# The y products of a pair of groups in the two halves of TensorE's columns, and GLU low parts built by DMA, in an S5 + MoBA trunk

## The chip, the core and the metric

The kernel runs on one core of one Trainium2 chip. The metric is the device time of one execution in microseconds. All times of rows are microseconds from the start of the profiled execution's span. PE is TensorE (PEld its weight loads), DVE is VectorE, ACT is ScalarE, POOL is GpSimd and SP is SyncE.

## The reference

A trunk of two layers over 256 tokens of width 1024. Each layer is a half-step SwiGLU FFN, a token mixer and a second half-step SwiGLU FFN, each with an RMSNorm ahead and a residual add. The mixer of layer 1 is an S5 state-space layer with 64 groups of 16 channels and 64 complex states; the mixer of layer 2 is block-sparse attention. The change lies in the S5 mixer:

```python
x_re, x_im = coef * (b @ u)                       # per group, complex
_, _, h_re, h_im = lax.associative_scan(combine, (abar, x), axis=1)
y = einsum('bsgp,gcp->bsgc', h_re, c_re) - einsum('bsgp,gcp->bsgc', h_im, c_im)
y = y.reshape(bsz, s, D_MODEL) + d_skip * u
y = gelu(y)
val, gate = split(y @ w_glu, 2, axis=-1)          # w_glu: 1024 x 2048
return val * sigmoid(gate)
```

## The kernel before

All large products are made in three parts: a weight w and an activation x are each split into a rounded part (hi, xh) and the rest (lo, xl), and `mm3` adds hi·xh, lo·xh and hi·xl. The weights lie in HBM as a row of granules of 128 x 1024 (512 KB), in the order in which they are used. `fetch` (line 162) takes the next granule: SP loads raw (L173), ACT rounds it to hi (L174), DVE subtracts to get lo (L175). hi and lo have four buffers each, raw has three. `take` hands a granule to the products and fetches so that three are ahead. Granules 66 to 81 hold w_glu: 66 to 73 are used in the S5 loop, one a pass, and 74 to 81 after it; the loop fetches 69 to 76.

The S5 mixer works on eight blocks b of eight groups. Time is cut in chunks of CL = 4 steps, NJ = 64 chunks. For a block:

- `s5_u`: ACT scales the rows into Hc (L845), PE transposes them to u (L853), ACT copies u in two halves to U (L858), and POOL's queue copies the two halves of the output matrices Om, swapped, to O2 (L861).
- `s5_x`: PE makes xst from U (L872); DVE multiplies with the tables Ct and St (L882 to L885), scans over the chunks (L888), and multiplies again to G1 and G2 (L891, L892).
- `s5_yu` and `s5_y`: PE adds up y, for each of the eight groups three f32 products of 128 rows and 64 columns, with Tm (L902), Om (L912) and O2 (L914). All write partitions 0 to 63 of a PSUM bank. ACT makes Yg from it with Gelu (L919).
- `s5_t`: PE transposes Yg to yT (L930); ACT makes xh of it (L934) and DVE xl (L938).

The blocks are staggered. A pass i of the loop does, on PE: yT of block i-2, xst of block i, y of block i-1, u of block i+1, and then the twelve GLU products of granule 64+i with block i-2. The order on PE and on SP is the order of the program text; ACT, DVE and POOL get theirs from a scheduler with priorities and a few written constraints (`issue_after`). Every engine works in its own order; tiles with few buffers make it wait for the last reader.

Of the kernel before, what the change touches and what calls it, by code (L numbers as in the profile page):

```python
# [10 lines left out]
F32 = mybir.dt.float32  # L11
F32R = mybir.dt.float32r
I32 = mybir.dt.int32
AF = mybir.ActivationFunctionType
ALU = mybir.AluOpType
# [12 lines left out]
GC = 16  # L28
NST = 64
CL = 4  # L30
NJ = SEQ // CL
# [4 lines left out]
PARTS = (2, 2)  # L36
WARM = (20, 2, 2, 8)
URGENT = 400


def ends(defer):
# [96 lines left out]
def yoco(ctx: ExitStack, tc: tile.TileContext, w, x, xt, ng, fg, sng, sd, sp, sb, sc, cst, out):  # L138
    nc = tc.nc
# [10 lines left out]
    def wbank(name):  # L150
        return psw.tile([128, 512], F32, tag="w", name=name)
# [8 lines left out]
    got, state = {}, {"n": 0, "use": 0, "bg": None, "end": NG, "credit": 0}  # L160

    def fetch():
        n = state["n"]
        if n >= NG:
            return
        state["n"] += 1
        raw = ring.tile([128, GR], F32, tag="raw", name="raw", bufs=3)
        hi = ring.tile([128, GR], F32R, tag="hi", name="hi")
        lo = ring.tile([128, GR], F32R, tag="lo", name="lo")
        step = 512 if n < 7 else GR  # L170
        for o in range(0, GR, step):
            s = slice(o, o + step)
            nc.sync.dma_start(raw[:, s], w[n][:, s])  # L173
            state["hi", n] = nc.scalar.activation(hi[:, s], raw[:, s], AF.Copy)  # L174
            state["lo", n] = nc.vector.tensor_tensor(lo[:, s], raw[:, s], hi[:, s].bitcast(F32), op=ALU.subtract)  # L175
        got[n] = (hi, lo)

# [64 lines left out]
    def xt_tiles(h, v=None):  # L242
        p, v = (xtp, "") if v is None else (v, "k")
        return (p.tile([128, 4, SEQ], F32R, tag=f"xh{h}{v}", name=f"xh{h}{v}", bufs=1),
                p.tile([128, 4, SEQ], F32R, tag=f"xl{h}{v}", name=f"xl{h}{v}", bufs=1))
# [7 lines left out]
    def split_scaled(dst, blk, src, gain):  # L253
        h, l = dst
        nc.scalar.activation(h[:, blk, :], src, AF.Copy, scale=gain)
        nc.vector.scalar_tensor_tensor(l[:, blk, :], src, gain, h[:, blk, :].bitcast(F32),  # L256
                                       op0=ALU.mult, op1=ALU.subtract)

    def transposed(xx, h, versions, bank=wbank):
# [11 lines left out]
        for dst, gi in dsts:  # L271
            for bp in range(2):
                for k in range(2):
                    blk = 2 * bp + k
                    with tc.high_priority(offset=URGENT if h else 0):
                        split_scaled(dst, blk, banks[bp][:, k, :], ngt[:, gi, 4 * h + blk:4 * h + blk + 1])
# [6 lines left out]
    def sumsq(ss, xx, h, urgent=False):  # L283
        with tc.high_priority(offset=URGENT if urgent else 0):
            for t in range(2):
                junk = small.tile([128, 512], F32, tag="junk", name="junk", bufs=1)
                nc.scalar.activation(junk, xx[t][h], AF.Square, accum_out=ss[:, 2 * h + t:2 * h + t + 1])
# [4 lines left out]
    def rnorm(ss, urgent=False, out=None):  # L292

        y = rnorm_tile() if out is None else out
        w_ = small.tile([128, 2, 3], F32, tag="rw", name="rw")
        with tc.high_priority(offset=URGENT if urgent else 0):
            for t in range(2):
# [15 lines left out]
    def rnorm_root(m, out, urgent=False):  # L313

        w_ = small.tile([128, 2], F32, tag="rw2", name="rw2")
        with tc.high_priority(offset=URGENT if urgent else 0):
            nc.vector.reciprocal(w_[:, 0:1], m)
# [6 lines left out]
    def ffn(pool, xx, lhs, r, head_mid, extra, tail_mid, tail, defer=DEFER, by_tile=False, late=False, then=None):  # L324
# [57 lines left out]
        def add(t, n, bank=None, c=slice(0, 512)):  # L382
            with tc.high_priority(offset=URGENT):
                src = acc[n][t] if bank is None else bank
                state["add"] = nc.vector.scalar_tensor_tensor(xx[t][n][:, c], src[:, c], 0.5, xx[t][n][:, c],  # L385
                                                              op0=ALU.mult, op1=ALU.add)
# [41 lines left out]
    with tc.manual_schedule(engines={PE, SP}):  # L428
# [5 lines left out]
        for i_ in range(4):  # L434
            raw = xn[i_ // 2][i_ % 2].rearrange("p (k t) -> p k t", k=2)
# [28 lines left out]
        Tm = smat.tile([128, CL, 32 * GC], F32, name="Tm")  # L464
        Om = smat.tile([128, G, CL, GC], F32, name="Om")
# [11 lines left out]
        H = [slice(0, 64), slice(64, 128)]  # L477
# [334 lines left out]


        sw = s5.enter_context(tc.tile_pool(name="sw", bufs=2))
        Gz = []
        for b in range(2):
            g1 = sw.tile([128, 8, NJ], F32, name=f"G1{b}", bufs=1)
            g2 = sw.tile([128, 8, NJ], F32, name=f"G2{b}", bufs=1)
            mt = sw.tile([128, 8, NJ], F32, name=f"Mt{b}", bufs=1)
            for t_ in (g1, g2, mt):  # L820
                nc.gpsimd.memset(t_[:, :, 0:1], 0.0)
            Gz.append((g1, g2, mt))

        Uz = []
        for b in range(3):
            u = sw.tile([128, 4, 2, NJ], F32, name=f"U{b}", bufs=1)
            nc.gpsimd.memset(u, 0.0)
            Uz.append(u)
        yT = [xt_tiles(h, sw) for h in range(2)]
        st = {}  # L830

        def s5_u(b):
            Hc = sw.tile([64, 8, CL, GC], F32, tag="Hc", name="Hc")
            hc = [None, None]
            for s_ in range(CL):
                t, sl = s_ // 2, s_ % 2
                src = xs[t][b // 4][64 * sl:64 * sl + 64, 128 * (b % 4):128 * (b % 4) + 128]
                rs = r[64 * sl:64 * sl + 64, t:t + 1]
                if b == 0 and s_ % 2:
                    hc[1] = V.tensor_scalar(Hc[:, :, s_, :], src.rearrange("p (g c) -> p g c", c=GC), rs, None, op0=ALU.mult)  # L840
                else:
                    with ExitStack() as order:
                        if b > 0:
                            order.enter_context(tc.issue_after(st[b - 1]["ins"]))
                        hc[0] = nc.scalar.activation(Hc[:, :, s_, :], src.rearrange("p (g c) -> p g c", c=GC), AF.Copy,  # L845
                                                     scale=rs)
            if b == 0:
                with tc.issue_after(hc[0].ins), tc.issue_after(hc[1].ins):
                    fetch()
            ub = wbank("u")  # L850
            uv = ub[:, 0:256].rearrange("p (q j) -> p q j", q=4)
            for q in range(4):
                nc.tensor.transpose(uv[:, q, :], Hc[:, 2 * q:2 * q + 2].rearrange("p g s c -> p (g s c)"),  # L853
                                    ident[0:64, 0:64])
            U = Uz[b % 3]
            for g2 in range(2):
                ps = slice(64 * g2, 64 * g2 + 64)
                done = nc.scalar.activation(U[ps, :, g2, :], uv[ps], AF.Copy)  # L858
            O2 = sw.tile([128, 8, CL, GC], F32, tag="O2", name="O2")
            for hh in range(2):  # L860
                nc.gpsimd.dma_start(O2[64 * hh:64 * hh + 64], Om[64 - 64 * hh:128 - 64 * hh, 8 * b:8 * b + 8])  # L861
            st[b] = {"U": U, "O2": O2, "ins": done.ins}

# [31 lines left out]
        def s5_yu(b):  # L895

            U = st[b]["U"]
            yb = wbank("y")
            st[b]["Y"] = Y = yb[0:64].rearrange("p (g f) -> p g f", g=8)
            for g in range(8):  # L900
                pr = 4 * b + g // 2
                nc.tensor.matmul(Y[:, g, :], U[:, g // 2, g % 2, :], Tm[:, :, GC * pr:GC * pr + GC],  # L902
                                 start=g == 0, stop=False)

        def s5_y(b, groups=range(8)):

            if "Y" not in st[b]:
                s5_yu(b)
            Y, O2 = st[b]["Y"], st[b]["O2"]
            g1, g2_, _ = Gz[b % 2]  # L910
            for g in groups:
                nc.tensor.matmul(Y[:, g, :], g1[:, g, :], Om[:, 8 * b + g].rearrange("p t c -> p (t c)"),  # L912
                                 start=False, stop=False)
                nc.tensor.matmul(Y[:, g, :], g2_[:, g, :], O2[:, g].rearrange("p t c -> p (t c)"),  # L914
                                 start=False, stop=g == 7)
            if groups[-1] < 7:
                return
            Yg = sw.tile([64, CL, 8, GC], F32, tag="Yg", name="Yg")
            nc.scalar.activation(Yg.rearrange("p t g c -> p g t c"), Y.rearrange("p g (t c) -> p g t c", c=GC),  # L919
                                 AF.Gelu_apprx_tanh)  # L920
            st[b]["Yg"] = Yg
            if b == 7:
                table(AF.Sigmoid, Yg[:, CL - 1, 7, GC - 1:GC])
# [21 lines left out]
        def last_t():  # L945
            with tc.high_priority(offset=URGENT):
                s5_t(7)
# [118 lines left out]
        for t in range(2):  # L1066
            nc.scalar.activation(ksb[:, t], kv[t][:, 0:256].rearrange("p (h d) -> p h d", h=KVH), AF.Copy,
                                 scale=r[:, t:t + 1])
            nc.scalar.activation(Vt[:, t], kv[t][:, 256:512].rearrange("p (h d) -> p h d", h=KVH), AF.Copy,
                                 scale=r[:, t:t + 1])  # L1070
# [203 lines left out]
```

## Time and profile before

| | us |
|---|---|
| median of 3 runs | 942.59 |
| lowest, highest | 942.35, 946.56 |
| the profiled execution, whole | 942.14 |
| its span | 940.4 |
| PE busy in it | 926.3 |
| DVE busy | 618.6 |
| ACT busy | 500.9 |

The span runs from the first to the last instruction that the profile shows; the profiled execution's time is 1.7 us longer. A product in f32 is two records on PE; one whose operands are rounded parts (fp32r) is one record.

### The profile page before, as it was taken

What the parts mean: (1) busy time and instruction counts of PE and PEld (TensorE: products, weight loads), DVE (VectorE), ACT (ScalarE), POOL (GpSimd) and SP (SyncE); (2) the same over time, 40 slices, a digit from 0 to 9 for tenths busy, and PEclk for the clock granted to TensorE, in tenths of its full rate; (3) what the DMA queues carried; (4) which work ended last, traced back from release to release, by engine and by line L of the source; (5) the groups of instructions that cost most, each with busy time, mean ns of one, the idle gap of its engine ahead of it and who ended that gap; (6) DMA issues with size and microseconds to landing.
All of it is one profiled execution on the core that took longest, in us unless ns stands there. A gap on an engine that the chain in (4) does not pass through costs nothing.

```text
span 940.4 us, 12472 instructions
## 1 busy us (share of the span) xinstructions
PE 926.3 (99%) x4610; PEld 766.7 (82%) x4610; DVE 618.6 (66%) x958; ACT 500.9 (53%) x742; POOL 41.8 (4%) x94
## 2 busy tenths in 40 slices
PE   9999999998999999999999999999999999999996
PEld 6788888887888888888888888888888888888885
DVE  7899988669976645555576555545578664555545
ACT  7544585566655544444466444444566654444444
POOL 0600000021100000000000000000000000000002
PEclk9999999999999999999999999999999999999999
DMA  8757555564335655555555555555552455555551
GB/s 300 229 195 225 186 185 196 168 208 148 118 98 184 195 187 192 182 196 183 183 179 189 183 185 193 187 184 194 183 178 76 160 186 188 187 190 188 188 186 66
DMA packets 49581, 169.93 MB, mean 181 GB/s; under 512 B 5936, under 2 KB 6368, under 8 KB 49520
## 3 DMA queue, kind: packets, MB, share of 16 engines
q1 hardware_dynamic: 46944, 162.33, 52.6%
q0 software_dynamic: 2144, 6.36, 2.4%
q8 instruction: 36, 0.59, 0.2%
q10 hardware_dynamic: 432, 0.45, 0.1%
q14 instruction: 25, 0.20, 0.1%
HBM read 164.46 MB, written 2.56 MB: 178 GB/s over the span
## 4 chain that ended last, share of the span: by engine, by line
PE 95%; DVE 2%; DMA 2%; ACT 1%; issue 0%; SPq 0%; ACTq 0%; DVEq 0%
PE pi L199 16%; PE pi L201 16%; PE pi L200 16%; PE acc L201 9%; PE acc L199 8%; PE acc L200 8%; PE gT L353 2%; PE glu L199 2%; PE glu L200 2%; PE glu L201 2%; DMA raw<-in_w 2%; PE xst L872 1%; PE q L201 1%; PE y L914 1%; PE y L912 1%; PE y L902 1%
## 5 line engine op out<-in xcount | busy, mean ns | idle before, releaser
L175 DVE TENSOR_TENSOR lo<-raw,hi 128x1024 fp32r<-128x1024 f32 (+1 forms) x307 | 368.7, 1202 | 270.0 <-ACT hi L174 269.4
L174 ACT ACTIVATE hi<-raw 128x1024 fp32r<-128x1024 f32 (+1 forms) x307 | 318.9, 1039 | 326.6 <-PE pi L201 180.4
L199 PE MATMUL pi<-hi,xh 128*128 128x512 f32 x704 | 279.2, 397 | 0.4 <-ACT hi L174 0.4
L201 PE MATMUL pi<-hi,xl 128*128 128x512 f32 x704 | 275.0, 391 | 0.0
L200 PE MATMUL pi<-lo,xh 128*128 128x512 f32 x704 | 274.3, 390 | 0.2
L201 PEld LDWEIGHTS pi<-hi,xl 128*128 128x128 f32 x704 | 132.1, 188 | 28.7 <-DVE xl L256 0.5
L199 PEld LDWEIGHTS pi<-hi,xh 128*128 128x128 f32 x704 | 132.3, 188 | 27.5 <-ACT hi L174 1.1
L200 PEld LDWEIGHTS pi<-lo,xh 128*128 128x128 f32 x704 | 132.4, 188 | 27.4 <-DVE lo L175 1.3
L201 PE MATMUL acc<-hi,gl 128*128 128x512 f32 x352 | 137.0, 389 | 1.0 <-DVE gl L357 1.0
L199 PE MATMUL acc<-hi,gh 128*128 128x512 f32 x352 | 137.8, 392 | 0.1
L200 PE MATMUL acc<-lo,gh 128*128 128x512 f32 x352 | 136.8, 389 | 0.0
L201 PEld LDWEIGHTS acc<-hi,gl 128*128 128x128 f32 x352 | 66.1, 188 | 15.3 <-DVE gl L357 1.6
L199 PEld LDWEIGHTS acc<-hi,gh 128*128 128x128 f32 x352 | 66.1, 188 | 13.8 <-ACT gh L356 0.5
L200 PEld LDWEIGHTS acc<-lo,gh 128*128 128x128 f32 x352 | 66.1, 188 | 13.4
L342 ACT ACTIVATE sl<-pi,ry 128x256 f32<-128x256 f32 x88 | 41.8, 475 | 50.3 <-PE pi L201 43.4
L343 DVE SCALAR_TENSOR_TENSOR g<-pi,ry,sl 128x256 f32<-128x256 f32 x88 | 42.0, 480 | 18.1 <-ACT sl L342 17.9
L1233 POOL TENSOR_TENSOR xg<-y,fgb 128x512 f32<-128x512 f32 (+1 forms) x5 | 5.3, 1064 | 657.7 <-DVE y L385 657.6
L357 DVE TENSOR_TENSOR gl<-gT,gh 128x512 fp32r<-128x512 f32 x44 | 30.1, 683 | 0.0
L353 PEld LDWEIGHTS gT<-ctile,g 128*128 128x128 f32 x176 | 21.8, 139 | 5.7
L353 PE MATMUL gT<-ctile,g 128*128 128x128 f32 x176 | 26.3, 272 | 0.0
L356 ACT ACTIVATE gh<-gT 128x512 fp32r<-128x512 f32 x44 | 25.6, 582 | 0.4 <-PE gT L353 0.4
L912 PE MATMUL y<-Om,G 128*64 128x64 f32 x128 | 15.8, 224 | 1.2 <-DVE G L891 1.2
(298 smaller groups left out, 830.5 us busy)
## 6 DMA issues: line engine op xcount, KB each, us to landing
raw<-in_w SPq DMA_DIRECT2D x293, 512.0 KB, 3.3
raw<-in_w SPq DMA_DIRECT2D x14, 256.0 KB, 4.9
O<-Om POOLq DMA_DIRECT2D x16, 128.0 KB, 2.5
y<-in_xt SPq DMA_DIRECT2D x4, 256.0 KB, 5.0
x<-in_x SPq DMA_DIRECT2D x4, 256.0 KB, 4.9
B<-in_sb POOLq DMA_DIRECT2D x4, 256.0 KB, 3.8
C<-in_sc POOLq DMA_DIRECT2D x4, 256.0 KB, 3.0
Tm<-KD POOLq DMA_DIRECT2D x2, 512.0 KB, 5.4
```

What stands on the lines that cost most here:

```text
L174: state["hi", n] = nc.scalar.activation(hi[:, s], raw[:, s], AF.Copy)
L175: state["lo", n] = nc.vector.tensor_tensor(lo[:, s], raw[:, s], hi[:, s].bitcast(F32), op=ALU.subtract)
L199: nc.tensor.matmul(bank, lh, wh, start=first, stop=False)
L200: nc.tensor.matmul(bank, lh, wl, start=False, stop=False)
L201: nc.tensor.matmul(bank, ll, wh, start=False, stop=last)
L342: nc.scalar.activation(sl, banks[t][:, 0:FC], AF.Silu, scale=r[:, t:t + 1])
L343: nc.vector.scalar_tensor_tensor(g, banks[t][:, FC:2 * FC], r[:, t:t + 1], sl, op0=ALU.mult, op1=ALU.mult)
L353: nc.tensor.transpose(bv[:, k, t * 128:t * 128 + 128], gs[t][:, k * 128:k * 128 + 128], ident)
L356: nc.scalar.activation(gh, bv, AF.Copy)
L357: nc.vector.tensor_tensor(gl, bv, gh.bitcast(F32), op=ALU.subtract)
L872: nc.tensor.matmul(xb[:, 128 * q:128 * q + 128], Sm[:, 4 * b + q, :], U[:, q].rearrange("p g j -> p (g j)"), start=True, stop=True)
L912: nc.tensor.matmul(Y[:, g, :], g1[:, g, :], Om[:, 8 * b + g].rearrange("p t c -> p (t c)"), start=False, stop=False)
```

## The change

The y products of the even groups of a block go to partitions 0 to 63 of the bank and those of the odd groups to partitions 64 to 127, which are the two halves of the array's columns. Their order alternates between the halves. Gelu is then two calls. For granules 69 to 76, lo is no longer made by DVE: ACT writes -raw, rounded, into lo, and POOL's queue adds the granule from HBM to it with an accumulating DMA. O2 gets a third buffer. The tiles of the stage are made in another order, and POOL's memsets get a higher priority.

```diff
+BY_DMA = {*range(69, 77)}
...
             nc.sync.dma_start(raw[:, s], w[n][:, s])
+            if n in BY_DMA:
+                nc.scalar.activation(lo[:, s], raw[:, s], AF.Copy, scale=-1.0)
+                nc.gpsimd.dma_start(lo[:, s], w[n][:, s], accum_op=ALU.add)
             state["hi", n] = nc.scalar.activation(hi[:, s], raw[:, s], AF.Copy)
+            if n in BY_DMA:
+                state["lo", n] = state["lo", n - 1]
+                continue
             state["lo", n] = nc.vector.tensor_tensor(lo[:, s], raw[:, s], hi[:, s].bitcast(F32), op=ALU.subtract)
...
+        yT = [xt_tiles(h, sw) for h in range(2)]
+        for z_ in ("M1", "M2", "Z"):
+            sw.tile([128, 8, NJ], F32, tag=z_, name=z_, bufs=1)
         Gz = []
...
-            for t_ in (g1, g2, mt):
-                nc.gpsimd.memset(t_[:, :, 0:1], 0.0)
+            with tc.high_priority(offset=2 * URGENT):
+                for t_ in (g1, g2, mt):
+                    nc.gpsimd.memset(t_[:, :, 0:1], 0.0)
...
-            nc.gpsimd.memset(u, 0.0)
+            with tc.high_priority(offset=2 * URGENT):
+                nc.gpsimd.memset(u, 0.0)
             Uz.append(u)
-        yT = [xt_tiles(h, sw) for h in range(2)]
...
-            O2 = sw.tile([128, 8, CL, GC], F32, tag="O2", name="O2")
+            O2 = sw.tile([128, 8, CL, GC], F32, tag="O2", name="O2", bufs=3)
...
-            st[b]["Y"] = Y = yb[0:64].rearrange("p (g f) -> p g f", g=8)
+            st[b]["Y"] = Y = [yb[h, 0:256].rearrange("p (q f) -> p q f", q=4) for h in H]
             for g in range(8):
                 pr = 4 * b + g // 2
-                nc.tensor.matmul(Y[:, g, :], U[:, g // 2, g % 2, :], Tm[:, :, GC * pr:GC * pr + GC],
-                                 start=g == 0, stop=False)
+                nc.tensor.matmul(Y[g % 2][:, g // 2, :], U[:, g // 2, g % 2, :], Tm[:, :, GC * pr:GC * pr + GC],
+                                 start=g < 2, stop=False)
...
-            for g in groups:
-                nc.tensor.matmul(Y[:, g, :], g1[:, g, :], Om[:, 8 * b + g].rearrange("p t c -> p (t c)"),
-                                 start=False, stop=False)
-                nc.tensor.matmul(Y[:, g, :], g2_[:, g, :], O2[:, g].rearrange("p t c -> p (t c)"),
-                                 start=False, stop=g == 7)
+            for q in range(4):
+                for g in (2 * q, 2 * q + 1):
+                    nc.tensor.matmul(Y[g % 2][:, q, :], g1[:, g, :], Om[:, 8 * b + g].rearrange("p t c -> p (t c)"),
+                                     start=False, stop=False)
+                for g in (2 * q, 2 * q + 1):
+                    nc.tensor.matmul(Y[g % 2][:, q, :], g2_[:, g, :], O2[:, g].rearrange("p t c -> p (t c)"),
+                                     start=False, stop=q == 3)
...
-            nc.scalar.activation(Yg.rearrange("p t g c -> p g t c"), Y.rearrange("p g (t c) -> p g t c", c=GC),
-                                 AF.Gelu_apprx_tanh)
+            for g2 in range(2):
+                nc.scalar.activation(Yg.rearrange("p t (q g) c -> g p q t c", g=2)[g2],
+                                     Y[g2].rearrange("p q (t c) -> p q t c", c=GC), AF.Gelu_apprx_tanh)
```

The y products of block 2 on PE, in the loop's second pass, before (G are the tiles G1 and G2, O is O2; the last two rows alternate for all eight groups):

```order
L930 MATMUL yT<-ctile,Yg 128x64 x4
L872 MATMUL xst<-U_2122,Sm 128x128 x4
L902 MATMUL y<-Tm,U_2126 64x64 x8
L912 MATMUL y<-Om,G_2110 64x64
L914 MATMUL y<-O_2296,G_2111 64x64
L912 MATMUL y<-Om,G_2110 64x64
```

The same place in the changed kernel:

```order
L944 MATMUL yT<-ctile,Yg 128x64 x4
L884 MATMUL xst<-U_2129,Sm 128x128 x4
L915 MATMUL y<-Tm,U_2133 64x64 x8
L926 MATMUL y<-Om,G_2117 64x64 x2
L929 MATMUL y<-O_2300,G_2118 64x64 x2
L926 MATMUL y<-Om,G_2117 64x64 x2
```

The products are the same in number; those of Om and of O2 now come in twos, one for each half of the columns, and nothing else on PE has moved.

One pass on ACT, before, from one Gelu to the next:

```order
L919 ACTIVATE Yg<-y 64x8x4x16
L858 ACTIVATE U_2124<-u 64x4x64 x2
L887 ACTIVATE Mt_2112<-m_173 128x8x63
L845 ACTIVATE Hc<-x_80,ry 64x8x16 x2
L845 ACTIVATE Hc<-x_82,ry 64x8x16 x2
L174 ACTIVATE hi<-raw 128x1024
L934 ACTIVATE xh0k<-yT 128x4x64
L919 ACTIVATE Yg<-y 64x8x4x16
```

The same pass in the changed kernel:

```order
L933 ACTIVATE Yg<-y 64x4x4x16 x2
L870 ACTIVATE U_2131<-u 64x4x64 x2
L899 ACTIVATE Mt_2119<-m_173 128x8x63
L857 ACTIVATE Hc<-x_80,ry 64x8x16 x2
L857 ACTIVATE Hc<-x_82,ry 64x8x16 x2
L176 ACTIVATE lo<-raw 128x1024
L178 ACTIVATE hi<-raw 128x1024
L948 ACTIVATE xh0k<-yT 128x4x64
```

The copy into lo stands ahead of hi, both ahead of xh, and Gelu is two calls. On DVE the row of lo is gone in each pass, and xl, which stood ahead of the next block's first three products with the tables, now stands behind the second of them.

The end of the loop on POOL's queue in the changed kernel (DMA rows are issues; fgb is the final norm's gain, which before stood right behind the last copy of Om):

```order
L177 DMA lo<-in_w 128x1024
L873 DMA O_2701<-Om 64x512 x2
L177 DMA lo<-in_w 128x1024 x3
L1228 DMA fgb<-in_fg 128x1024
L177 DMA lo<-in_w 128x1024
```

The last row is granule 76. POOL's memsets, which stood behind the first two blocks' copies of Om, now stand ahead of them.

## Rows read from the trace of the kernel before

**Rows 1.** The page: the span, the busy time of each engine with its share of the span and its instructions, and the shares of the chain that ended last.

```profile
span 940.4 us, 12472 instructions
PE 926.3 (99%) x4610; PEld 766.7 (82%) x4610; DVE 618.6 (66%) x958; ACT 500.9 (53%) x742; POOL 41.8 (4%) x94
...
PE 95%; DVE 2%; DMA 2%; ACT 1%; issue 0%; SPq 0%; ACTq 0%; DVEq 0%
```

**Rows 2.** Busy time of each engine in the passes of the loop, cut at the first GLU product of each: from and to, length, busy time of each engine (with its instructions), granted clock, share of time that the DMA engines were busy, GB/s.

```profile
core 0: us, PE busy (x) PEld busy (x) DVE busy (x) ACT busy (x) POOL busy (x), PEclk, DMA share, GB/s
...
225.89:233.80 7.91, 7.91 (x79) 6.74 (x77) 7.78 (x11) 5.00 (x11) 1.03 (x3) 1.00 0.70 212
233.80:241.57 7.77, 7.77 (x78) 6.66 (x76) 7.63 (x11) 5.05 (x11) 1.02 (x3) 1.00 0.51 155
...
249.33:257.08 7.75, 7.75 (x78) 6.66 (x76) 6.92 (x10) 5.07 (x11) 1.03 (x3) 1.00 0.37 107
257.08:264.44 7.36, 7.36 (x74) 6.34 (x72) 6.71 (x10) 3.34 (x6) 1.01 (x2) 1.00 0.34 102
264.44:270.74 6.30, 6.30 (x67) 5.38 (x65) 5.49 (x7) 2.18 (x3) 0.00 (x0) 1.00 0.09 36
```

**Rows 3.** The timeline of PE in one pass: start, time covered, line, operation, out<-in, the array's shape, shapes, number of records.

```profile
249.33 0.50 PE L199 MATMUL glu<-hi,xh0k 128*128 128x512 f32 x1
...
252.27 0.46 PE L930 MATMUL yT<-ctile,Yg 64*128 64x64 f32 x4
252.66 1.16 PE L872 MATMUL xst<-U,Sm 128*128 128x128 f32 x8
253.75 1.15 PE L902 MATMUL y<-Tm,U 128*64 128x64 f32 x16
254.73 0.28 PE L912 MATMUL y<-Om,G 128*64 128x64 f32 x2
...
256.48 0.28 PE L914 MATMUL y<-O,G 128*64 128x64 f32 x2
256.69 0.46 PE L853 MATMUL u<-ctile,Hc 64*128 64x64 f32 x4
```

**Rows 4.** The timeline of ACT in the same pass; in brackets the idle time before a row and what ended it.

```profile
249.10 0.59 ACT L919 ACTIVATE Yg<-y 64x512 f32<-64x512 f32 x1 [2.57 <-PE y L914]
249.60 0.76 ACT L858 ACTIVATE U<-u 64x256 f32<-64x256 f32 x2
...
252.56 1.06 ACT L174 ACTIVATE hi<-raw 128x1024 fp32r<-128x1024 f32 x1
253.64 0.66 ACT L934 ACTIVATE xh1k<-yT 128x256 fp32r<-128x256 f32 x1
256.86 0.59 ACT L919 ACTIVATE Yg<-y 64x512 f32<-64x512 f32 x1 [2.56 <-PE y L914]
```

**Rows 5.** The timeline of DVE in the same pass: the granule's lo.

```profile
253.65 1.22 DVE L175 TENSOR_TENSOR lo<-raw,hi 128x1024 fp32r<-128x1024 f32 x1 [0.70 <-ACT hi L174]
```

**Rows 6.** The timeline of PE's weight loads: of the kern products (128 stationary columns, 32 moving ones) while the S5 matrices are built, of one GLU product, and of the y products with Tm.

```profile
122.60 1.99 PEld L697 LDWEIGHTS kern<-CC,E 128*128 128x128 f32 x16
...
249.44 0.19 PEld L200 LDWEIGHTS glu<-lo,xh0k 128*128 128x128 f32 x1
...
253.75 1.01 PEld L902 LDWEIGHTS y<-Tm,U 128*64 128x64 f32 x16
```

**Rows 7.** The timeline ahead of the loop, all engines.

```profile
207.29 1.48 POOL L827 MEMSET U<- 128x512 f32 x3
...
208.14 0.40 ACT L845 ACTIVATE Hc<-x,ry 64x128 f32<-64x128 f32 x1 [0.81 <-DVE ry L310]
208.14 0.70 DVE L840 TENSOR_SCALAR Hc<-x,ry 64x128 f32<-64x128 f32 x1
...
224.55 0.33 PE L914 MATMUL y<-O,G 128*64 128x64 f32 x2
...
225.51 0.46 PE L853 MATMUL u<-ctile,Hc 64*128 64x64 f32 x4
```

**Rows 8.** The timeline at the end of the loop: the last GLU product of granule 71, hi of granule 75, xh of block 6, the first GLU product of granule 72, hi of granule 76, the sigmoid, and the first product that reads lo of granule 76.

```profile
267.09 0.39 PE L201 MATMUL glu<-hi,xl1k 128*128 128x512 f32 x1
...
267.51 1.06 ACT L174 ACTIVATE hi<-raw 128x1024 fp32r<-128x1024 f32 x1 [2.31 <-PE glu L201]
...
268.48 0.62 ACT L934 ACTIVATE xh1k<-yT 128x256 fp32r<-128x256 f32 x1
...
270.74 0.50 PE L199 MATMUL glu<-hi,xh1k 128*128 128x512 f32 x1
...
274.41 1.06 ACT L174 ACTIVATE hi<-raw 128x1024 fp32r<-128x1024 f32 x1 [0.88 <-PE glu L201]
...
276.47 1.28 ACT L986 ACTIVATE sg<-glu 128x512 f32<-128x512 f32 x2 [1.00 <-PE glu L201]
...
282.93 0.39 PE L200 MATMUL glu<-lo,xh0k 128*128 128x512 f32 x1
```

**Rows 9.** DMA issues by line: out<-in, queue, number, KB each, median us from issue to landing.

```profile
O<-Om POOLq DMA_DIRECT2D x16, 128.0 KB, 2.5
...
Tm<-KD POOLq DMA_DIRECT2D x2, 512.0 KB, 5.4
...
fgb<-in_fg POOLq DMA_DIRECT2D x1, 512.0 KB, 5.0
```

More of the change, by code (lines that the diff above doesn't have):

```diff
@@ L898, in s5_yu, with s5_y @@
             yb = wbank("y")
-            st[b]["Y"] = Y = yb[0:64].rearrange("p (g f) -> p g f", g=8)
+            st[b]["Y"] = Y = [yb[h, 0:256].rearrange("p (q f) -> p q f", q=4) for h in H]
             for g in range(8):
                 pr = 4 * b + g // 2
-                nc.tensor.matmul(Y[:, g, :], U[:, g // 2, g % 2, :], Tm[:, :, GC * pr:GC * pr + GC],
-                                 start=g == 0, stop=False)
-        def s5_y(b, groups=range(8)):
+                nc.tensor.matmul(Y[g % 2][:, g // 2, :], U[:, g // 2, g % 2, :], Tm[:, :, GC * pr:GC * pr + GC],
+                                 start=g < 2, stop=False)
+        def s5_y(b):
             if "Y" not in st[b]:
@@ L910, in s5_y @@
             g1, g2_, _ = Gz[b % 2]
-            for g in groups:
-                nc.tensor.matmul(Y[:, g, :], g1[:, g, :], Om[:, 8 * b + g].rearrange("p t c -> p (t c)"),
-                                 start=False, stop=False)
-                nc.tensor.matmul(Y[:, g, :], g2_[:, g, :], O2[:, g].rearrange("p t c -> p (t c)"),
-                                 start=False, stop=g == 7)
-            if groups[-1] < 7:
-                return
+            for q in range(4):
[5 more added lines that the diff above has]
+                                     start=False, stop=q == 3)
             Yg = sw.tile([64, CL, 8, GC], F32, tag="Yg", name="Yg")
-            nc.scalar.activation(Yg.rearrange("p t g c -> p g t c"), Y.rearrange("p g (t c) -> p g t c", c=GC),
-                                 AF.Gelu_apprx_tanh)
+            for g2 in range(2):
+                nc.scalar.activation(Yg.rearrange("p t (q g) c -> g p q t c", g=2)[g2],
+                                     Y[g2].rearrange("p q (t c) -> p q t c", c=GC), AF.Gelu_apprx_tanh)
             st[b]["Yg"] = Yg
```

## The prediction

> **What bounds the kernel now.** I read the page first, then one stage of it more and more closely. The page [rows 1] shows TensorE (PE) busy for 926.3 us of a span of 940.4 us, and 95% of the chain that ended last lies on PE. So time is won only where PE's stream gets shorter, and only as far as no other engine then holds PE up. The change touches one stage, the S5 loop and the little ahead of it. Cut at the first GLU product of each pass [rows 2], the loop shows a first pass of 7.91 us, three alike of 7.77 to 7.75 (the middle one is left out), one of 7.36 and one of 6.30 us, PE busy for the whole of each, at a granted clock of 1.00. VectorE (DVE) follows closely with 7.78 to 5.49 us, ScalarE (ACT) has 5.07 us in a full pass. The loop is PE-bound, with DVE less than a microsecond behind.
>
> One pass on PE [rows 3] reads: twelve GLU products from 249.33, the yT transposes at 252.27, xst at 252.66, the y products from 253.75, the u transposes at 256.69. The 24 y products are 48 records (each f32 product is two): 16 in the Tm row at 253.75, 32 from 254.73 to the pair at 256.48, whose second record ends its place about 0.06 later and leaves the drain before u. That is 2.85 us for 48 records, 59 ns each. ACT in the same pass [rows 4] works without a gap from Yg at 249.10 to the end of xh at 254.30, 5.20 us, and is then idle 2.56 us until y is done. DVE [rows 5] spends 1.22 us on the granule's lo, after waiting 0.70 us for hi.
>
> **The y products.** What sets the 59 ns? The kern product [rows 6] streams only 32 columns but has 128 stationary ones, and its 16 loads take (1.99 - 0.19) / 15 = 120 ns each; y has 64 stationary columns and (1.01 - 0.14) / 15 = 58 ns. The pace goes by the columns loaded, and y loads and uses one half of the array (the shape reads 128*64) while the other half stands still. After the change neighbouring products go to different halves. The two records of one product stay on one half, but the second of one product can run beside the first of the next. No row of before shows two halves at work at once, so the gain has two bounds: nothing, if the halves take their loads in turn (59 ns a record still), or half of 2.85 us, 1.42 us a pass, if they work side by side. I take the second: half of the columns is unused in all 48 records, and a load already runs beside a product (the load at 249.44 lies under the product at 249.33 that lasts 0.50 us [rows 3, 6]), so nothing in these rows makes a load own the whole array. PE's pass would be 7.75 - 1.42 = 6.33 us.
>
> The Trainium skill speaks against this. Its page "TensorE: Matmul & The Clock Gate", section "Part 3: Packing small matmuls — row/col tiling", says that a weight load overlaps products in flight only if the row groups differ; the two halves here share all rows. By that rule the gain is 0 and the kernel stays at 942 us. Read strictly it would also forbid the load at 249.44, which has the same rows as the product above it, so the trace bears it out only in part; "TensorEngine Tiling (Array Packing)", section "Key Properties", says on the contrary that different tiles load and multiply in parallel, which would give the 1.42 us. No run here shows either yet.
>
> **ACT and DVE.** ACT gets the first step of lo, a copy of the shape of hi, 1.06 us. Yg (64x512, 0.59 us) becomes two calls of 64x256; the nearest row is U, two calls of 64x256 in 0.76 us, so +0.17 us (bounds: 0 and +0.59, two calls as long as the old one). ACT's gapless stretch becomes 5.20 + 1.06 + 0.17 = 6.43 us, at most 6.85. DVE loses 1.22 us: 6.92 - 1.22 = 5.70 us. That saves nothing by itself, since PE hid it; but had it stayed, DVE would hold the pass at 6.9 us. So the pass comes to max(6.33, 6.43, 5.70) = 6.43 us: ACT takes over as the bound by a hair. One more wait is to be looked at: xh stands behind lo and hi on ACT, and the next GLU products need it. Like hi now, lo waits for raw and for the end of the GLU products of four granules ago, whose buffer it takes; hi at 267.51 starts right at that end (267.09 + 0.39 [rows 8]). So xh ends some 2.9 us after yT has begun (0.1 + 1.06 + 1.06 + 0.66); PE gets to GLU again after yT, xst, y and u, 0.39 + 1.09 + 1.43 + 0.39 = 3.3 us after yT began. It fits, by 0.4 us. DVE's xl now stands behind two of the next block's products, and ends about when the third GLU record wants it: a tenth of a microsecond at most.
>
> **The sum over the loop.** Pass one: 7.91 - 6.43 = 1.48. The three full passes: 7.75 - 6.43 = 1.32 each, 3.96. The fifth has no Hc on ACT (3.34 us + 1.23 [rows 2]), so PE sets it: 1.42. In the sixth PE has neither xst nor u, and ACT is late: hi starts at 267.51 and xh ends at 269.10 [rows 8]; with lo ahead it ends at 270.16, so GLU starts about 270.26 instead of 270.74: 0.48. Together 7.34 us.
>
> **Before the loop.** The memsets now come ahead of the copies into O2. In before, POOL's memset of U lies at 207.29 to 208.77 and DVE's Hc at 208.14 takes 0.70 us [rows 7], where ACT needs 0.40 for the same shape. u needs both: without the overlap it follows ACT's Hc (end 208.54) instead of DVE's (208.84): 0.3 us. After that DVE sets the pace up to the last G of block 1; from the O products at 224.55 to u at 225.51 about 14 records become 7: 0.4 us. O2's third buffer and the earlier tiles cost nothing: these copies are issued well over a pass ahead.
>
> **The low parts by DMA.** Each is 512 KB through POOL's queue; the nearest row is fgb, same size and queue, 5.0 us [rows 9]. An accumulating transfer also reads its destination; I bound it by 5.0 and by twice that, 10 us, and take 7.5. POOL's queue is in order: each lo issue waits for ACT, and an O2 copy waits behind it that is wanted more than a pass later. In the loop a granule is used about three passes after its lo, over 15 us, so nothing shows. The tight one is granule 76: its lo waits for GLU of granule 72, as hi did at 274.41, ends on ACT at 275.47, and PE wants the sum at 282.93 [rows 8]: 7.46 us for the transfer. 5.0 us: no wait; 10 us: 2.5 us. With 7.5 us: 0. The doubled ACT work there delays the first sigmoid from 276.47 to 276.53 or so: -0.1 us. SP's raw loads now wait for hi, 252.56 + 2 x 1.06 = 254.68 in this pass, where they waited for DVE's lo, 254.87 [rows 4, 5]: 0.
>
> Sum: 7.34 + 0.3 + 0.4 - 0.1 = 7.9 us. The profiled execution took 942.14 us, so 934.2; the median of the three runs stands 0.45 us higher: 934.7. With PE, ACT and DVE so close that some joints will leak a few hundredths each pass, I say **935.0 us**.
>
> **Rivals.** *The halves take turns* (the change doesn't do what it says): PE still needs 7.75 us a pass, DVE's relief is hidden, only 0.3 us before the loop remains: 942 us. For it: no row with two halves. *Half a gain*: records start 45 ns apart, say, because the closest starts of records anywhere in these rows are the 58 ns of y, and something below half of that may bind: 48 x 14 ns = 0.67 us a pass, 4 us, and 0.5 before: 938 us. *The accumulating transfer is slow* (the slower side): its place is granule 76, its price is its duration less 7.46 us. With the halves side by side it eats the whole gain from 15 us on and makes the kernel slower by over 0.5% from 20 us; if the halves take turns, from 12 us. Beyond about 17 us every pass would wait too. At 20 us, 947 to 952 us. Against it: the copies on that queue take 2.5 to 5.4 us [rows 9], and the DMA engines are busy for 0.34 to 0.37 of the later passes [rows 2].
>
> **How the numbers follow.** Side by side: 0.50, own range 932.5 to 937. Half a gain: 0.15. Taking turns: 0.22. Slow transfer: 0.13. The range leaves out the slow transfer and the last few in a hundred below: 932.5 to 943.5. A measurement of this kernel tells 0.5%, 4.7 us, from no change. Below 937.9 lie the first case and the better part of the second: 0.63 faster. Same: turns and the rest of the second, 0.25. Slower: 0.12.
>
> **What would show it.** Right: y records of a pass cover about 1.4 us instead of 2.85, passes of 6.4 to 6.5 us, ACT without its 2.56 us gap, PE with small gaps before GLU. Wrong: y pairs still 0.115 us apart in start (turns), or waits of PE's lo products for the POOL queue, at granule 76 first (slow transfer), or ACT's Yg calls at 0.59 us each, which would give passes of 6.85 us and some 937 us.

## The result and the profile after

| | before | after |
|---|---|---|
| median, us | 942.85 (5 runs, 942.35 to 946.56) | 936.78 (5 runs, 934.61 to 937.4) |
| the profiled execution, whole | 942.14 | 935.26 |
| its span | 940.4 | 933.5 |

The ratio is 0.9925, 95% interval 0.9913 to 0.9938: faster by 0.75%. The forecast was 935.0 us; 936.78 lies inside the range, 1.8 us above the forecast.

The page after, to be held against [rows 1]:

```profile
span 933.5 us, 12494 instructions
PE 919.7 (99%) x4610; PEld 759.2 (81%) x4610; DVE 608.8 (65%) x950; ACT 510.1 (55%) x758; POOL 47.4 (5%) x102
...
PE 97%; DVE 1%; ACT 1%; DMA 0%; issue 0%; ACTq 0%; DVEq 0%
```

PE is busy for 6.6 us less and the span is 6.9 us shorter. DVE lost 9.8 us, ACT gained 9.2. The passes, cut as in [rows 2]; the last row is the sixth pass:

```profile
core 0: us, PE busy (x) PEld busy (x) DVE busy (x) ACT busy (x) POOL busy (x), PEclk, DMA share, GB/s
226.06:232.44 6.38, 6.38 (x78) 5.26 (x77) 5.04 (x8) 6.22 (x13) 2.13 (x5) 1.00 0.91 205
232.44:239.05 6.61, 6.61 (x78) 5.27 (x76) 6.42 (x10) 6.29 (x13) 2.01 (x4) 1.00 1.05 298
239.05:245.56 6.51, 6.51 (x78) 5.19 (x77) 6.05 (x9) 6.29 (x13) 2.02 (x4) 1.00 0.98 262
245.56:251.91 6.35, 6.35 (x78) 5.23 (x76) 5.73 (x9) 6.20 (x13) 2.00 (x3) 1.00 0.91 211
251.91:258.00 6.09, 6.09 (x74) 4.87 (x72) 5.79 (x9) 4.59 (x8) 0.89 (x1) 1.00 0.93 181
258.00:263.75 5.75, 5.44 (x68) 4.05 (x65) 4.49 (x7) 3.40 (x5) 0.86 (x1) 1.00 0.78 177
```

The six passes take 37.69 us; before they took 44.85 [rows 2]. That is 7.16 us, and so the whole gain. The third of them on PE, and the weight loads of its Tm products:

```profile
242.15 0.46 PE L944 MATMUL yT<-ctile,Yg 64*128 64x64 f32 x4
242.53 1.16 PE L884 MATMUL xst<-U,Sm 128*128 128x128 f32 x8
243.62 0.69 PE L915 MATMUL y<-Tm,U 128*64 128x64 f32 x16
244.14 0.29 PE L926 MATMUL y<-Om,G 128*64 128x64 f32 x4
244.25 0.29 PE L929 MATMUL y<-O,G 128*64 128x64 f32 x4
...
245.17 0.46 PE L865 MATMUL u<-ctile,Hc 64*128 64x64 f32 x4
```

```profile
243.62 0.55 PEld L915 LDWEIGHTS y<-Tm,U 128*64 128x64 f32 x16
```

From the first y product to u it is 1.55 us; in [rows 3] it was 2.94. Four records now take the 0.115 us that two took, and the 16 loads of Tm 0.55 us instead of 1.01 [rows 6]. The rows around it have kept their lengths: xst to y is 1.09 us here and there. ACT in the same pass:

```profile
238.84 0.77 ACT L933 ACTIVATE Yg<-y 64x256 f32<-64x256 f32 x2 [0.16 <-PE y L929]
...
242.61 1.06 ACT L176 ACTIVATE lo<-raw 128x1024 fp32r<-128x1024 f32 x1
243.57 1.04 ACT L178 ACTIVATE hi<-raw 128x1024 fp32r<-128x1024 f32 x1
244.64 0.64 ACT L948 ACTIVATE xh0k<-yT 128x256 fp32r<-128x256 f32 x1
245.35 0.77 ACT L933 ACTIVATE Yg<-y 64x256 f32<-64x256 f32 x2
```

The idle 2.56 us of [rows 4] are gone: the copy into lo lies in them, and from Yg to Yg the timeline marks no idle time.

Ahead of the loop stands something that the prediction does not have. The rows are the 8 us before the first pass, first of the profiled execution, then of another one of the same kernel:

```profile
218.00:220.00 2.00, 2.00 (x37) 1.75 (x38) 1.94 (x6) 0.76 (x2) 0.83 (x2) 0.74 0.03 12
220.00:222.00 2.00, 0.88 (x7) 0.69 (x6) 1.88 (x5) 1.72 (x4) 0.20 (x1) 0.50 0.55 131
222.00:224.00 2.00, 2.00 (x14) 1.78 (x15) 1.86 (x5) 1.94 (x6) 0.00 (x0) 0.50 0.00 0
224.00:226.00 2.00, 2.00 (x36) 1.87 (x32) 1.99 (x5) 1.98 (x3) 0.81 (x2) 0.55 0.03 8
```

```profile
218.00:220.00 2.00, 1.99 (x40) 1.63 (x40) 1.94 (x6) 1.01 (x3) 0.90 (x2) 1.00 0.00 0
220.00:222.00 2.00, 0.89 (x9) 0.76 (x7) 1.88 (x5) 1.91 (x5) 0.13 (x1) 1.00 0.55 131
222.00:224.00 2.00, 1.20 (x20) 0.83 (x18) 1.86 (x5) 1.94 (x5) 0.00 (x0) 1.00 0.00 0
224.00:226.00 2.00, 1.78 (x22) 1.44 (x23) 1.99 (x5) 1.96 (x4) 1.25 (x3) 1.00 0.04 8
```

In the first the granted clock falls to 0.50, the lower of PE's two levels (1.2 instead of 2.4 GHz), after a stretch in which PE waited for DVE (from 214 to 218 us it was busy for 2.07 of 4.00 us; before, for 2.59). In the second it stays at 1.00, although PE was busy for only 2.14 us in the same stretch. What makes it fall in one execution and not in the other no run here shows. The run `after_again` below is about this.

### The profile page after: what moved, and what is told of

It reads as the page before. It is cut to its first block, busy times and chain, and to the rows that moved or that the text cites. A ratio compares the mean times of both kernels' runs of the same rounds, so it can differ in the third digit from the quotient of the medians.

```text
span 933.5 us, 12494 instructions
## 1 busy us (share of the span) xinstructions
PE 919.7 (99%) x4610; PEld 759.2 (81%) x4610; DVE 608.8 (65%) x950; ACT 510.1 (55%) x758; POOL 47.4 (5%) x102
## 3 DMA queue, kind: packets, MB, share of 16 engines
HBM read 168.66 MB, written 2.56 MB: 183 GB/s over the span
## 4 chain that ended last, share of the span: by engine, by line
PE 97%; DVE 1%; ACT 1%; DMA 0%; issue 0%; ACTq 0%; DVEq 0%
PE pi L206 17%; PE pi L208 17%; PE pi L207 17%; PE acc L208 9%; PE acc L206 9%; PE acc L207 9%; PE gT L360 2%; PE glu L206 2%; PE glu L208 2%; PE glu L207 2%; PE xst L884 1%; PE q L208 1%; PE oacc L208 1%; PE oacc L206 1%; PE q L207 1%; PE oacc L207 1%
## 5 line engine op out<-in xcount | busy, mean ns | idle before, releaser
L182 DVE TENSOR_TENSOR lo<-raw,hi 128x1024 fp32r<-128x1024 f32 (+1 forms) x299 | 358.4, 1200 | 267.8 <-ACT hi L178 267.3
L262 ACT ACTIVATE xh<-xT,ngt 128x256 fp32r<-128x256 f32 x32 | 14.0, 468 | 5.2 <-DVE xl L263 3.5
```

## Experiments

**The columns alone.** The y products in two halves, but lo by DVE.

```diff
-BY_DMA = {*range(69, 77)}
+BY_DMA = set()
```

> The changed kernel with DVE making the low parts of granules 69 to 76 again; the y products stay in the two halves. Theory (the halves work side by side, and then DVE's lo would hold the pass): y of a pass takes 1.45 us as in the changed kernel, but DVE, which was idle for only about 2.2 us in the first five passes of before (passes of 38.55 us in all, DVE busy for 36.3), becomes the bound: passes of 7.7 to 6.9 us with DVE busy throughout, PE waiting for G ahead of y. Gain over before some 2.2 us in five passes and 0.5 in the sixth: about 940 us. Rival (DVE's relief is worth nothing, the columns carry all): 936.8 us, as the changed kernel, with passes of 6.5 us.

Measured: 940.02 us (5 runs, 939.19 to 941.38), ratio 0.9964 (0.9952 to 0.9977). The first pass and two full ones:

```profile
226.50:235.04 8.54, 8.54 (x78) 6.89 (x77) 7.55 (x10) 4.84 (x10) 0.80 (x3) 0.72 0.65 214
...
241.40:248.40 7.00, 6.74 (x78) 5.43 (x76) 6.87 (x10) 5.34 (x12) 1.02 (x3) 1.00 0.41 112
248.40:255.37 6.97, 6.71 (x78) 5.43 (x76) 6.84 (x10) 5.34 (x12) 1.02 (x2) 1.00 0.39 115
```

DVE fills the full passes and PE has gaps. (In the first, the granted clock is 0.72: the fall seen above, which here reaches into the loop.) The forecast's "had it stayed, DVE would hold the pass at 6.9 us" is right. The columns alone give about half of the gain (3.2 us of 6.1).

**The low parts alone.** The y products as before, lo by the transfer; the diff undoes the hunks on y and Yg.

> The changed kernel with the y products and Gelu as before (one half of the columns, eight groups in a row); lo of granules 69 to 76 stays with ACT and the accumulating transfer. Theory: PE stays the bound with passes of 7.75 us and y of 2.85 us; only the 0.3 us ahead of the loop are won: 942.5 us. Rival one (the transfers slow the loop: the copies into O2 now land in 7.8 instead of 2.5 us and raw in 6.6 instead of 4.3): over 944 us, with waits of PE for lo or for O2. Rival two (DVE's relief is a gain by itself): under 940.5 us.

Measured: 942.4 us (11 runs, 941.89 to 945.07), ratio 0.9994 (0.9985 to 1.0003): no difference that can be told. A pass:

```profile
241.85:249.60 7.75, 7.75 (x78) 6.66 (x77) 6.13 (x9) 5.99 (x12) 2.00 (x4) 1.00 0.83 184
```

PE is busy throughout, DVE's relief lies under it, and the additional traffic costs nothing. So the two parts, each with the earlier memsets, are worth 3.2 us and 0.8 us apart (the second with an interval from 1.4 us faster to 0.3 us slower) and 6.1 us together: DVE's relief pays only after PE's.

**One half after the other.** Only the order differs: of Tm all even groups first, then the odd ones; of Om and O2, of every two pairs the even groups first, then the odd ones.

```diff
...
-            for q in range(4):
-                for g in (2 * q, 2 * q + 1):
...
+            for g in (0, 2, 1, 3, 4, 6, 5, 7):
+                q = g // 2
```

> The changed kernel with all its tiles and places, only the order of the y products altered: the even groups of a pair of pairs (one half of the columns) come first, then the odd ones, instead of even and odd by turns. Theory (the gain comes from neighbouring products on different halves running side by side): most records follow one on the same half, 59 ns each, y of a pass takes about 2.6 to 2.85 us, passes 7.5 to 7.75 us, and the time is 941.5 to 942.5 us. Rival (the place of the outputs or the DMA part brings the gain, not the order): y of 1.45 us and 936.8 us.

Measured: 937.76 us (5 runs, 937.45 to 940.32), ratio 0.9945 (0.9933 to 0.9958). Neither number; by the time alone it can hardly be told from the changed kernel, whose interval overlaps. The timeline of PE can tell them apart and shows why:

```profile
244.32 0.79 PE L915 MATMUL y<-Tm,U 128*64 128x64 f32 x13
244.90 0.27 PE L926 MATMUL y<-Om,G 128*64 128x64 f32 x1
244.95 0.22 PE L915 MATMUL y<-Tm,U 128*64 128x64 f32 x1
245.00 0.22 PE L926 MATMUL y<-Om,G 128*64 128x64 f32 x1
...
246.37 0.46 PE L865 MATMUL u<-ctile,Hc 64*128 64x64 f32 x4
```

In the program all sixteen Tm records stand ahead of the first Om record. On the chip the first half begins with Om at 244.90 while the second half still has Tm records to come. Each half works through its own records 58 ns apart, and PE hands on some that stand behind records of the other half. With eight records in a row, y takes 2.05 us (more than 1.55, less than 2.94) and the first four passes 6.86 to 6.89. So the theory was right on what runs side by side and wrong on how strictly the halves have to alternate. A new theory with a number (some three records ahead) goes into the next run.

**Long runs on a half.** For blocks 2 to 7 all twelve even products, then all twelve odd ones, 24 records in a row.

```diff
...
+            for g in (0, 2, 1, 3, 4, 6, 5, 7) if b < 2 else (0, 2, 4, 6, 1, 3, 5, 7):
+                q = g // 2
+                if b >= 2 and g == 1:
+                    for k in (1, 3, 5, 7):
...
```

> The changed kernel with the y products of blocks 2 to 7 in two long runs: all twelve products of the even groups (24 records) on one half, then all twelve of the odd groups on the other; blocks 0 and 1 as in the run with the halves one after the other. In that run, with eight records in a row on a half, every half kept its own pace of 58 ns and the next half's first record started while the last three of the half before were still to come, so eight records took five places of 58 ns: 2.05 us a pass. Theory (PE hands on a few records of the next half ahead, some three, and no more): 48 records take about 45 places, 2.6 to 2.7 us a pass, passes of 7.5 to 7.6 us, 941.3 us (940.8 to 942). Rival (each half works through its own products freely, however far apart they stand in the program): y of 1.5 us as in the changed kernel, 936.5 to 937 us.

Measured: 941.44 us (11 runs, 940.9 to 943.77), ratio 0.9982 (0.9973 to 0.9991). PE's timeline; L929 is Tm of the odd groups, which stands behind the last O2 of the even ones (L933):

```profile
248.28 0.68 PE L915 MATMUL y<-Tm,U 128*64 128x64 f32 x8
...
249.49 0.22 PE L931 MATMUL y<-Om,G 128*64 128x64 f32 x1
249.50 0.27 PE L929 MATMUL y<-Tm,U 128*64 128x64 f32 x1
249.55 0.22 PE L931 MATMUL y<-Om,G 128*64 128x64 f32 x1
249.60 0.22 PE L929 MATMUL y<-Tm,U 128*64 128x64 f32 x1
...
251.04 0.46 PE L865 MATMUL u<-ctile,Hc 64*128 64x64 f32 x4
```

The second half starts when three or four records of the first are left, and the two overlap only there. y takes 2.76 us, passes 7.57 and 7.58. The theory holds: PE reaches a few records ahead, and a long run on one half leaves 0.18 of the 1.39 us a pass that y had gained. Of the time, 1.70 us of the 7.35 that the changed kernel gains on the same chip are left.

**More warm products.** The kernel before already has some products without use ahead of the loop (`warm`), which only fill PE's time. This run has eleven more, in idle places of PE there.

```diff
             s5_x(1, PARTS[1])
-            s5_y(0)
+            warm(3, *idle)
+            s5_y(0, 4)
...
+                if i_ == 2:
+                    warm(4, *idle)
```

(The 4 in `s5_y(0, 4)` is the number of warm products between its halves.)

> The changed kernel with eleven more products without use, 128x512 each, in three idle places of PE ahead of the loop (three before the y products of block 0, four between its halves, four ahead of xst of block 2), 0.23 us each. In the changed kernel PE's granted clock falls to 0.50 from about 218 to 225.5 us, after a stretch in which PE was busy for half of the time; xst of block 2 takes 2.08 instead of 1.13 us there. Theory (the missing 0.57 us of the forecast for this stretch is the clock's): clock 1.00 from 204 to 226 us, the first GLU product 0.6 us sooner, 936.2 us, and the five runs lie closer together than the 2.8 us of the changed kernel. Rival one (DVE sets the pace there whatever the clock): 936.8 us. Rival two (the added products hold up the chain from u to xst): 937 us or more.

Measured: 935.71 us (4 runs, 934.62 to 936.35), ratio 0.9916 (0.9902 to 0.993). That looked like the theory, but the changed kernel's 936.78 comes from another set of runs. So both were run on one chip:

> The changed kernel once more, beside the kernel with more warm products on the same chip. Theory (the clock that falls ahead of the loop costs about 0.6 us, and more where it rises later): median about 936.8 us, executions with a mean clock of 0.993 to 0.995 longer by 1 us or more than those with 0.998, and about 1 us over the kernel with more warm products. Rival (the difference between the two in the first comparison was that of the chips): both within 0.4 us.

> The kernel with more warm products once more, beside the changed kernel on the same chip. Theory: 935.7 us, mean clock 0.996 to 0.999 in all executions, about 1 us under the changed kernel. Rival (a difference of the chips): no difference over 0.4 us.

Measured: the changed kernel 935.79 us (5 runs, 934.95 to 936.88), with more warm products 936.27 (5 runs, 935.01 to 938.34), ratios 0.9923 and 0.9927. The 1 us is not there: the medians stand 0.5 us apart the other way, their intervals overlap, and the runs with more warm products lie no closer together. But the clock theory holds within the executions. Time in us and mean granted clock of each execution of the changed kernel, both comparisons, sorted by clock:

```
0.998: 934.61  934.95  935.79    0.997: 935.59
0.995: 936.78    0.994: 935.26    0.993: 937.05  937.40  936.88    0.992: 936.47
```

Of what is missing to 1, 0.001 to 0.003 falls behind PE's last product. The six with 0.995 or less, of which the profiled one is one, average 936.64 us, the four others 935.24. From the first warm product to the first GLU product the traces show 21.63 us before, 21.49 in the profiled execution after (clock fallen), and 20.94 in `after_again`, in `e4_more_warm_products` and in `e4_again` (clock held; 20.95 in the last).

So the fall is an event that comes or not. A mean of 0.995 or less stands in 12 of 31 executions with the y products in both halves and without more warm products (the changed kernel 6 in 10, the columns alone 3 in 5, one half after the other 1 in 5, long runs 2 in 11), in 4 of 50 with all y products in one half (before 4 in 39, the low parts alone 0 in 11) and in none of 13 with more warm products (with the next run). Left out are the three runs further below whose traces show falls in other places too. It came more often where PE idled more ahead of the loop. Its price depends on how long it lasts. In the profiled execution it ended ahead of the first GLU product and cost 0.55 us. In that of the long runs it lasted to about 229.4 us: up to the first GLU product this took 23.14 us where the run with one half after the other, the same program up to there, took 21.21; the first pass took 8.11 us where the next three took 7.57 or 7.58; and the whole took 943.77, where the nine executions without the fall lie from 940.9 to 941.97.

In the traces with added work on PE the clock holds ahead of the loop, but the work bought nothing: the 13 executions average 935.99 us, 0.75 above the four of the changed kernel whose clock held, and the five of `e4_again` spread over 3.3 us at 0.997 and 0.998. So the times spread for another reason too, which stays open, and the 1.4 us between the two groups go with the fall but are not its price alone.

**Granule 76 by DVE.** `BY_DMA = {*range(69, 76)}`, on top of the warm products.

> The kernel with more warm products, and DVE makes the low part of granule 76 again (69 to 75 stay with the transfer). In the changed kernel's trace the transfer for 76 is issued at 268.73, lands 7.0 us later and is wanted at 276.10, so 0.4 us are left. Theory (it fits, in all runs): the same as the kernel with more warm products alone, within 0.3 us. Rival (in the slower executions this transfer is late, and that is part of the spread): 0.3 to 1 us less in the median and a smaller spread.

Measured: 935.68 us (4 runs, 935.55 to 936.04), ratio 0.9919 (0.9905 to 0.9932). Within 0.6 us of both runs with warm products; the runs lie closer together, but four are too few to make that a finding. It is the lowest median of all kernels here, and not to be told from the changed kernel's 935.79 on the same chip.

**The transfer of granule 76 twice.**

```diff
                 nc.gpsimd.dma_start(lo[:, s], w[n][:, s], accum_op=ALU.add)
+                if n == 76:
+                    nc.gpsimd.dma_start(lo[:, s], w[n][:, s], accum_op=ALU.add)
```

> The changed kernel in which the accumulating transfer of granule 76 alone is made twice, one after the other (its low part then holds one weight too many, so that this granule's contribution is wrong). Theory (the transfers are free only because the granule is wanted later; the price is duration less what is left, and granule 76 is the tight place): 7.0 us and again 7 to 8 us with its issue, less the 7.4 us between issue and use: PE waits some 7 us ahead of the first lo product of granule 76 and nowhere else, 943 to 944 us. Rival (something else hides the end of the loop, or the order in which PE takes the products can step over it): under 940 us.

Measured: 947.76 us (4 runs, 946.49 to 948.6), ratio 1.0046 (1.0031 to 1.0061). The wait, from the list of waits from 270 to 300 us, and the time around it:

```profile
PE glu L209 <- DMA lo<-in_w: 7.9, 1, 7.9
```

```profile
280.00:285.00 5.00, 0.00 (x0) 0.00 (x0) 0.83 (x1) 0.00 (x0) 0.00 (x0) 0.68 0.86 198
285.00:290.00 5.00, 3.42 (x8) 2.77 (x9) 0.00 (x0) 0.00 (x0) 0.00 (x0) 0.50 0.32 113
290.00:295.00 5.00, 5.00 (x19) 4.00 (x19) 1.22 (x1) 1.40 (x2) 0.00 (x0) 0.80 0.00 2
```

The place is as expected, and the price nearly: one wait, 7.9 us instead of some 7, at granule 76. The time is 4 us above the expectation, because the wait has a second price: PE idles, its granted clock falls to 0.50, and the first twelve GLU records after the wait come 0.44 us apart instead of 0.23, 2.5 us more. The profiled execution also has the fall ahead of the loop (0.50 from 224 to 230 us). With 936.64 us for the changed kernel with a fallen clock, 7.9 + 2.5 gives 947.0.

**-raw on POOL, -raw on DVE.** To see whether ACT holds the pass, its 1.06 us went to POOL and to DVE (both on top of the run with granule 76 by DVE).

```diff
-                nc.scalar.activation(lo[:, s], raw[:, s], AF.Copy, scale=-1.0)
+                nc.gpsimd.tensor_scalar(lo[:, s], raw[:, s], -1.0, None, op0=ALU.mult)
```

> The kernel with more warm products and 76 by DVE, where the first step of the low parts of 69 to 75 (-raw into lo) is made by POOL, which is idle for most of a pass, instead of ACT (1.06 us a pass). Its first five passes there are 6.47, 6.72, 6.55, 6.37 and 6.08 us. Theory (ACT is the bound by a hair, PE comes next at 6.33): passes of 6.33 to 6.4 us, 0.6 to 0.9 us less in all, about 935 us. Rival one (PE is already the bound): passes as they are within 0.05 us, no change of the time. Rival two (POOL's work on 128x1024 slows DVE, which then holds the pass): passes over 6.7 us and 937 us or more.

> The same, but -raw is made by DVE: one operand of rounded-off f32 instead of the two of the old subtraction (1.22 us). Theory (DVE has 0.6 to 0.7 us to spare in a pass of 6.4 us): if a copy of one operand takes about half of 1.22 us, the passes stay at 6.35 to 6.5 us and the time at 935.3 us; if it takes 1.1 us as on ACT, DVE holds the pass at 6.8 us and the time is 937.5 us. Rival (DVE's waits, not its busy time, hold the pass in either case): as the run with the columns alone, passes of 7 us.

Measured: POOL 937.31 us (5 runs, 936.84 to 938.51), ratio 0.9941 (0.9929 to 0.9954); DVE 938.48 us (5 runs, 937.33 to 939.11), ratio 0.9951 (0.9938 to 0.9963). Both are slower than the run on which they stand. With POOL (its own row, then a DVE row that overlaps it, then ACT):

```profile
243.33 2.86 POOL L176 TENSOR_SCALAR lo<-raw 128x1024 fp32r<-128x1024 f32 x1 [1.35 <-PE glu L207]
```

```profile
243.66 1.33 DVE L903 TENSOR_TENSOR G<-Z,Ct 128x504 f32<-128x504 f32 x1
```

```profile
246.78 0.77 ACT L935 ACTIVATE Yg<-y 64x256 f32<-64x256 f32 x2 [1.03 <-PE y L929]
```

POOL needs 2.86 us, and the G product that starts just behind POOL's row takes 1.33 instead of 0.68 us; the two DVE rows after it, still within POOL's, keep their 0.67 and 0.68. ACT now has 1.03 us to spare, but passes two to four are 6.47, 6.56 and 6.51 us, where they were 6.72, 6.55 and 6.37. The loss is in the first pass (7.96 us instead of 6.47; in the profiled execution the clock is fallen from its start to about 229.7 us, although the warm products are there) and in the sixth (6.51 instead of 5.74), where PE waits 0.93 us for the longer G. The clock is not all of it: the two executions with a mean of 0.998 took 936.84 and 937.31 us. So none of the three expectations came. With DVE (a full pass and the sixth, then PE in the sixth):

```profile
239.62:246.14 6.52, 6.52 (x78) 5.35 (x76) 6.39 (x10) 5.36 (x12) 2.03 (x4) 1.00 1.04 288
...
258.63:265.53 6.90, 5.35 (x69) 4.14 (x65) 6.33 (x10) 2.47 (x4) 1.63 (x2) 1.00 0.84 171
```

```profile
263.97 0.34 PE L926 MATMUL y<-Om,G 128*64 128x64 f32 x4 [1.29 <-DVE G L903]
```

Passes two to four stay at 6.44 to 6.52 us with ACT relieved and DVE at 6.39. The copy took 0.69 us, about half of 1.22, and these passes are as expected for that, but the time is 3.2 us over the 935.3 expected. The loss is in the sixth pass (6.90 us instead of 5.74), where PE waits 1.29 us for DVE's G, which stands behind -raw there, in the first (6.97 instead of 6.47) and, in the profiled execution, in a clock at 0.50 that follows the sixth. Neither run relieves ACT without loading DVE or slowing it, so which of the three engines binds stays open to 0.1 us. But with ACT off the path no pass of the first four gets under 6.44 us, and the changed kernel's own first and fourth take 6.38 and 6.35, with PE busy throughout.

## Why the prediction was right

- **The halves work side by side: right.** 1.42 us a pass was forecast, 2.94 - 1.55 = 1.39 came. The rule of the Trainium skill, "TensorE: Matmul & The Clock Gate", section "Part 3: Packing small matmuls — row/col tiling", that a weight load overlaps products in flight only if the row groups differ, and by which the gain was 0, does not hold for these two halves, which share their rows: 1.55 us instead of 2.94. What the Trainium skill says in "TensorEngine Tiling (Array Packing)", section "Key Properties", that different tiles load and multiply in parallel, is borne out by the same number, with a bound that the two runs on order show: only for products that stand near each other (2.05 us with eight records in a row on a half, 2.76 with 24).
- **The pass: right in size.** 6.43 us forecast; the four full ones average 6.46. That ACT takes over "by a hair" is not shown: the fourth took 6.35 us, less than the 6.43 at which ACT was to hold it, and freeing ACT bought nothing. PE's own 6.35 and its wait for xl give the same mean, so that 6.43 fits so well is partly luck.
- **The loop's sum: right to 0.2 us.** First pass 1.53 (forecast 1.48), the next three 3.81 (3.96), the fifth 1.27 (1.42), the sixth 0.55 (0.48): 7.16 against 7.34. The joints that were to leak do so in the GLU products, whose third record waits for xl: twelve take 3.10 us in the pass from 239.05, 2.94 in [rows 3], where a tenth at most was forecast. The weight load of that third record, in this pass and at granule 72:

```profile
239.65 0.19 PEld L208 LDWEIGHTS glu<-hi,xl0k 128*128 128x128 f32 x1 [0.30 <-DVE xl0k L952]
...
264.40 0.19 PEld L208 LDWEIGHTS glu<-hi,xl1k 128*128 128x128 f32 x1 [0.35 <-DVE xl1k L952]
```

  So another 0.17 us goes at granules 72 and 73, whose products run from 263.75 to 270.30 (6.55 us; 6.38 before). The forecast took off 0.1 there, but for the sigmoid, which waits for PE as before.
- **Ahead of the loop: right while the clock holds.** 0.3 + 0.4 forecast, 21.63 - 20.94 = 0.69 shown. In the profiled execution 0.14 is left of it. The run with the low parts alone, which has the memsets but not the columns, shows 21.39: 0.24 of the 0.3.
- **The transfer: right, with less to spare than it sounds.** 7.5 us was taken, halfway between two bounds. The eight landed in 7.0 to 9.7 us from issue, 7.6 in the middle, and raw and O2 became slower beside them (O2 from 2.5 [rows 9] to 7.8) without a wait on PE. The last one, its issue on POOL's queue and the first product that reads it:

```profile
268.73 0.87 POOL L177 DMA_DIRECT2D lo<-in_w  x1 [4.29 <-ACT lo L176]
```

```profile
276.10 0.39 PE L207 MATMUL glu<-lo,xh0k 128*128 128x512 f32 x1
```

  It landed 7.0 us after its issue, 0.4 us before it was read. At the 9.7 us of the second granule it would have cost 2.3. In the other traces that have this transfer once it landed in 6.6 to 7.4 us, so the last one was not quick by luck in this execution alone. The price "its duration less 7.46 us" was confirmed by the doubled transfer, except that it leaves out what an idle PE does to the clock. One sum of that rival is a little off: with the halves taking turns the kernel would be 0.5% slower from 12.7 us on (942 + 12.7 - 7.46 = 947.2), not from 12.
- **What the forecast missed** is the clock ahead of the loop. For executions in which it held, 934.7 was worked out (935.0 with leaks) and 935.24 is their mean; in those in which it fell, 936.64. The first comparison had four of the second kind in five. The sum had taken PE's time at 1.00 because [rows 2] and the whole stage of before stood at 1.00; it did not ask what a PE that waits longer there does to that.

## What to carry to other kernels

Products that need half of the columns can be put side by side in the two halves and take about half the time (here 1.55 us instead of 2.94), if the program lets the halves alternate every few records. Before the pacing engine is shortened, see which engine stands next: here the first part was worth 3.2 us by itself, the second 0.8 us, not to be told from nothing, and the two together 6.1. Where work was taken off PE in a stretch in which it waits already, its clock fell more often, so the time of such a stretch has to be worked out at both levels.

## What the runs showed of the hardware

- PE starts products out of the program's order when they lie on different column halves: the Om record at 244.90 ahead of Tm records at 244.95. In the two runs on order it reaches only some three records far: eight in a row on a half give 2.05 us for 48 records, 24 in a row 2.76, two in a row 1.55.
- POOL takes 2.8 to 3.2 us for a 128x1024 multiplication by -1 that ACT does in 1.06 and DVE in 0.69, and the DVE product that starts just behind it goes from 0.68 to 1.33 us.
- An accumulating transfer of 512 KB into SBUF lands in 6.6 to 9.8 us. In the changed kernel's full passes the view gives the DMA engines a busy share of 0.91 to 1.05.
- A wait of 7.9 us on PE costs about 2.5 us more, through twelve records at a granted clock of 0.50 after it.
